# A hybrid streaming layer on one core: the sample tile's stage cut into twelve steps, and each tile's output transpositions placed behind the next tile's state product

## The chip, the core and the metric

The kernel runs on one core of a Trainium2 chip. A core has five engines that each work through a list of instructions of their own, in order: PE (TensorE, the matmuls), DVE (VectorE), ACT (ScalarE), POOL (GpSimd) and SP (SyncE, which here only issues DMAs). They wait for one another by semaphores. The metric is the device time of one execution in microseconds (us); the time of a kernel is the median of its runs.

## What is computed

One layer of a streaming encoder over 2048 prompt frames (16 tiles of 128) and 8 running streams of 16 frames (one more tile, number 16, the sample tile), width 1024, in float32. Cut to what matters here:

```python
h   = rmsnorm(x, norm_mix_pre)
P   = h @ w_in          # -> q|k|v (3*512), z (512), b (4), a (4), B, C, H (512 each)
qkv = silu(causal_dwconv(P[qkv], conv_prev, conv_qkv_w))      # 4 taps, 4 heads x 128
beta, g = sigmoid(b), -exp(a_log) * softplus(a + dt_bias)
# gated delta rule, in chunks: (I + A) is unit lower triangular
A   = strict_lower(kb @ k.T * decay)
u, w = solve(I + A, [v * beta, kb * exp(g)])
# along the chunks of a stream, with the state S (128 x 128 per head):
v_new = u - w @ S
o   = (q * exp(g)) @ S + (q @ k.T * decay) @ v_new
S   = S * exp(g_last) + k_tail.T @ v_new
o   = rmsnorm(o, gdn_norm_w) * silu(z)
y   = B * causal_dwconv(C * H)                                # 3 taps
x   = x + rmsnorm(concat(o, y) @ w_o)
x   = x + rmsnorm((silu(h2 @ w_gate) * (h2 @ w_up)) @ w_down) # h2 = rmsnorm(x)
```

The prompt's tiles carry S from one to the next; the sample tile has eight states of its own.

## The kernel before

**Phases.** The span has four: the w_in phase (0 to about 970 us), the w_o phase, gate and up (L1010), and down (L1168). The change is in the first.

**Groups.** The w_in phase takes the tiles in six groups, numbered 0 to 5: [0, 1, 16], [2, 3, 4], [5, 6, 7], [8, 9, 10], [11, 12] and [13, 14, 15]. Each goes through 28 projections (`project`, the matmuls at L139): one projection multiplies the group's tokens (384 columns, 256 in group 4) with one 128-wide slice of w_in, in 24 matmuls, since both sides are split into a `hi` and a `lo` part. Projections are counted through here, 0 to 167: group 1 has 28 to 55, and so on. In a group 0 to 11 give k, v, q (`qkv_stage`), 12 to 15 z (`z_stage`) and 16 to 27 the C, H and B of the short convolution (`sc_stage`).

**What a group does beside its projections.** `x_prep` takes the next group's x, gets each token's root mean square, spreads it over the partitions with a matmul with ones (`spread`, L179) and makes the eight pairs `hi` (ScalarE, L209) and `lo` (VectorE, L206 and L210). `gate_prep` makes b and a (the 16-wide matmuls with `wba`, also L139). `pair_stage` makes k k^T and q k^T per tile (L519, L520) and then the solve: 31 steps of two VectorE instructions (L539, L541) on all the group's 32-blocks at once; the result goes to DRAM (L542) and comes back in another layout (`utd`). `level_stage` builds the larger blocks out of it (PE at L568 to L595). `chunk_stage` does a prompt tile: S.k (L625), U.r (L632), the new state (L639), q.S (L646), qk.y (L651). `sample_stage` does the sample tile, head by head: L677, L679, L684, L687 and L693 on PE. Both end in `out_stage`: o is normalized (L612), transposed by PE (L615) and multiplied with `sz`, the SiLU of z, into `ot` (L617).

**What sets the order.** The program is traced in the order of the code, and a scheduler then puts each engine's list in order from its own estimate of times, with what was traced earlier first. All the stages of a group behind its k, v, q thus run among the projections of the next group. The engines keep that order on the chip.

**Walls.** Three PSUM banks hold projections (`dbank`), two the pair, level, chunk and sample products (`gbank`), one the q.S, qk.y and output transpositions (`obank`). `sz` has one buffer. A group's z projections 12 to 14 therefore fill the three banks and wait there until the last `out_stage` of the group before has read `sz`; the projection after them (projections 43, 71, 99, 127, 155 and the ones that follow each) cannot start sooner. The xk tiles, which also serve `rg` in `spread` and `bsb` in `gate_prep`, have four buffers.

## Time and profile before

| | |
|---|---|
| Time, median of 3 runs | 2603.46 us (2603.07 to 2608.24) |
| Profiled execution, its own time | 2609.88 us |
| Its span | 2608.1 us |
| Granted TensorE clock, mean over the span | 0.987 |
| PE busy | 2509.2 us (96%), in 15129 matmul records |
| VectorE busy | 1748.9 us (67%) |
| ScalarE busy | 1033.2 us (40%) |
| GpSimd busy | 645.1 us (25%) |

The span is one execution under the profiler, from its first instruction to its last, and the execution's own time is 1.8 us longer. [...]

### The profile page before, as it was taken

To read this page: it belongs to the slowest core of one execution; us is meant where nothing else is said; L and a number is where in the kernel's file an instruction comes from. 1 tells how busy PE (TensorE), PEld (TensorE's weight loads), DVE (VectorE), ACT (ScalarE), POOL (GpSimd) and SP (SyncE) were. 2 spreads that over 40 slices of the span, in tenths; PEclk is the share of its full clock that TensorE was granted. 3 is DMA by queue.
4 is the path that set the end of the run, shared out by engine and by line. 5 is a ranking of instruction groups with operands and counts; after the bars stand their busy time and mean duration, and the time that the engine had idled before them with its cause. 6 is when DMAs were issued, how large, how long until landed. Compare 5 with 4: busy or idle time off the path is not lost.

```text
span 2608.1 us, 41962 instructions
## 1 busy us (share of the span) xinstructions
PE 2509.2 (96%) x15129; PEld 2337.4 (90%) x15129; DVE 1748.9 (67%) x3549; ACT 1033.2 (40%) x2496; POOL 645.1 (25%) x598
## 2 busy tenths in 40 slices
PE   8989999999989999999999999999999999999998
PEld 7989899999888988778999999999999988788786
DVE  7787766666587665777878864544655555677598
ACT  6545144261554423444434442222433335333343
POOL 3321101010120101214556620000000025555563
PEclk9999999999999999999999999999999999999999
DMA  7876575757567573768877788887988853443466
GB/s 266 297 267 238 193 268 198 246 193 237 193 205 247 184 233 129 234 216 287 291 253 271 264 281 259 280 246 244 295 272 296 275 176 106 125 125 122 128 216 185
DMA packets 320816, 589.42 MB, mean 226 GB/s; under 512 B 55533, under 2 KB 204721, under 8 KB 301793
## 3 DMA queue, kind: packets, MB, share of 16 engines
q1 hardware_dynamic: 182512, 509.28, 58.8%
q10 hardware_dynamic: 138096, 77.46, 9.8%
q8 instruction: 120, 1.97, 0.3%
q14 instruction: 88, 0.71, 0.1%
HBM read 424.60 MB, written 162.05 MB: 225 GB/s over the span
## 4 chain that ended last, share of the span: by engine, by line
PE 70%; DVE 11%; DMA 9%; ACT 4%; issue 3%; POOL 2%; ACTq 1%; SPq 0%; DVEq 0%; POOLq 0%
PE fbank L1010 32%; PE dbank L139 15%; PE fbank L1168 10%; PE tbank L794 3%; PE dbank L794 3%; DMA xk<-in_xT 1%; DVE xr L1187 1%; DMA dr<-in_w_dn 1%; DVE acc L370 1%; DMA xt<-in_x 1%; DVE acc L1127 1%; DMA w<-wsplit 1%; DVE Ts L541 1%; DMA partd<-pt 1%; DMA utd<-sT 1%
## 5 line engine op out<-in xcount | busy, mean ns | idle before, releaser
L1010 PE MATMUL fbank<-xh,fw 128*128 128x384 f32 (+1 forms) x3696 | 901.3, 327 | 9.4 <-ACT m L1044 4.4
L139 PE MATMUL dbank<-hi,w 128*128 128x384 f32 (+1 forms) x2688 | 685.3, 334 | 12.7 <-ACT w L342 6.0
L1010 PEld LDWEIGHTS fbank<-xh,fw 128*128 128x128 f32 x3696 | 653.2, 188 | 11.3 <-ACT m L1044 5.0
L1010 PE MATMUL fbank<-xl,fw 128*128 128x384 f32 (+1 forms) x1848 | 603.7, 327 | 0.0
L139 PEld LDWEIGHTS dbank<-hi,w 128*128 128x128 f32 x2688 | 480.8, 191 | 18.5 <-ACT w L342 6.0
L1168 PE MATMUL fbank<-dw,as 128*128 128x512 f32 x1980 | 458.8, 393 | 8.6 <-DVE acc L1127 2.5
L1168 PEld LDWEIGHTS fbank<-dw,as 128*128 128x128 f32 x1980 | 370.6, 188 | 96.5 <-DVE acc L1127 4.5
L139 PE MATMUL dbank<-lo,w 128*128 128x384 f32 (+1 forms) x1344 | 446.4, 332 | 1.1 <-DVE lo L228 1.1
L1010 PEld LDWEIGHTS fbank<-xl,fw 128*128 128x128 f32 x1848 | 348.1, 188 | 0.0
L139 PEld LDWEIGHTS dbank<-lo,w 128*128 128x128 f32 x1344 | 256.9, 191 | 3.7 <-DVE lo L228 1.7
L1152 POOL TENSOR_TENSOR as<-ar,as 128x256 fp32r<-128x256 f32 (+1 forms) x207 | 186.5, 911 | 277.7 <-ACT as L1149 276.9
L1127 DVE TENSOR_TENSOR acc<-acc,fbank 128x512 f32<-128x512 f32 x248 | 166.3, 682 | 93.4 <-PE fbank L1168 75.6
L867 POOL TENSOR_TENSOR dw<-dr,dw 128x512 fp32r<-128x512 f32 x52 | 77.3, 1498 | 484.6 <-ACT dw L865 484.4
L1149 ACT CAST as<-ar 128x256 fp32r<-128x256 f32 (+1 forms) x288 | 117.8, 427 | 181.3 <-PE fbank L1168 130.0
L985 ACT CAST fw<-rg 128x512 fp32r<-128x512 f32 x124 | 77.3, 623 | 188.9 <-PE fbank L1010 170.8
L370 DVE SCALAR_TENSOR_TENSOR acc<-R,cw,acc 128x384 f32<-128x384 f32 (+2 forms) x216 | 132.8, 620 | 12.8 <-ACT acc L401 8.8
L344 POOL TENSOR_TENSOR w<-wr,w 128x512 fp32r<-128x512 f32 x49 | 73.0, 1490 | 228.0 <-ACT w L342 170.5
L1057 DVE TENSOR_TENSOR c<-u,fbank 128x384 f32<-128x384 f32 (+1 forms) x66 | 34.9, 529 | 102.2 <-PE fbank L1010 102.0
L1053 DVE TENSOR_TENSOR m<-m,m 128x384 f32<-128x384 f32 (+1 forms) x44 | 23.1, 525 | 97.8 <-ACT m L1046 97.8
L539 DVE TENSOR_TENSOR pr<-As,Ts 48x31 f32<-48x31 f32 (+25 forms) x186 | 66.7, 359 | 29.8 <-DMA As<-sa 25.7
L342 ACT CAST w<-wr 128x512 fp32r<-128x512 f32 x98 | 56.4, 616 | 61.9 <-PE dbank L139 29.4
L1055 ACT ACTIVATE m<-fbank 128x384 f32<-128x384 f32 (+1 forms) x66 | 31.2, 473 | 121.5 <-PE fbank L1010 112.4
(358 smaller groups left out, 3708.3 us busy)
## 6 DMA issues: line engine op xcount, KB each, us to landing
w<-wsplit SPq DMA_DIRECT2D x119, 1024.0 KB, 5.3
fw<-fsplit SPq DMA_DIRECT2D x188, 512.0 KB, 4.8
fsplit<-fw SPq DMA_DIRECT2D x94, 512.0 KB, 4.0
partd<-pt ACTq DMA_DIRECT2D x88, 384.0 KB, 6.5
rg<-in_w_gu SPq DMA_DIRECT2D x62, 512.0 KB, 4.3
wsplit<-w SPq DMA_DIRECT2D x28, 1024.0 KB, 5.3
wr<-in_w_in SPq DMA_DIRECT2D x98, 256.0 KB, 3.9
ar<-partd SPq DMA_DIRECT2D x48, 384.0 KB, 3.3
```

Source lines behind the costliest of these rows:

```text
L139: T.matmul(ps, l, r, start=(i == 0), stop=(i == n - 1))
L344: e.tensor_tensor(out=wl[:, c], in0=wr, in1=wh[:, c].bitcast(F32), op=ALU.subtract)
L370: V.scalar_tensor_tensor(acc, raw(d), w[:, d:d + 1], acc, op0=ALU.mult, op1=ALU.add)
L539: V.tensor_mul(p3, As[:m, j, j + 1:32].unsqueeze(2).broadcast_to([m, a, b]), Ts[:m, j, 0:b].unsqueeze(1).broadcast_to([m, a, b]))
L794: T.matmul(pss[n], m_[:, j, :], w_[k][:, n * 512:(n + 1) * 512], start=(k == 0 and ci == 0), stop=(k == KD - 1 and ci == 2))
L867: e.tensor_tensor(out=w[:, 1], in0=v, in1=w[:, 0].bitcast(F32), op=ALU.subtract)
L985: A.copy(w[:, 0], v)
L1010: T.matmul(ps, w_[:, c], b_[k][:, :hw], start=(first and k == 0 and ci == 0), stop=(k == KH - 1 and ci == 2), skip_group_check=not first)
L1127: V.tensor_add(dst, dst, ps)
L1149: ins = A.copy(a[:, 0, :n], v)
L1152: e.tensor_tensor(out=a[:, 1, :n], in0=v, in1=a[:, 0, :n].bitcast(F32), op=ALU.subtract)
L1168: T.matmul(ps, a[:, x_, q * P:(q + 1) * P], w[:, y_], start=(start and q == 0 and ci == 0), stop=(q == c - 1 and ci == 2), skip_group_chec ...
```

## The change

Three things. `x_prep` becomes a generator that is stepped between the projections of `sc_stage`, so that its instructions are traced among them and not behind them. `sample_stage` becomes a generator with three stops per head; its twelve steps are traced behind the first twelve projections of the next group, where before all of it stood in its own group behind `z_stage`. And a tile's `out_stage` is traced behind the next tile's state product, with PE's first transposition ordered behind that product (`issue_after`); the last tile's stands behind the first projection of `sc_stage`. The x and xk loads are ordered behind the same weight loads as before (`w0 + 11`, `w0 + 20`), xk now one load ahead. No instruction is added or taken away on any engine.

```diff
-        def x_prep(tiles):
+        def x_prep(tiles, got, w0):
...
                         A.activation(xt, xt, AF.Square, accum_out=ss[:, i:i + 1])
+                    yield
...
             rb = spread(r, n)
...
+            load()
+            yield
+            load()
             for k in range(KD):
...
+                got.append((h, l))
+                load()
+                yield
...
             fetch()
+            if steps and j < 12:
+                next(steps[0], None)
             return ps
...
             for h in range(H):
-                T.transpose(ps[:, h * P:(h + 1) * P], o[:, h, :], ident)
+                with tc.issue_after(after.ins) if after is not None and h == 0 else ExitStack():
+                    T.transpose(ps[:, h * P:(h + 1) * P], o[:, h, :], ident)
...
-                T.matmul(ps[:, h * P:(h + 1) * P], kl[:, h, :], yt[:, h, :], start=True, stop=True)
+                last = T.matmul(ps[:, h * P:(h + 1) * P], kl[:, h, :], yt[:, h, :], start=True, stop=True)
...
+            for f in outs:
+                f(last)
             ps = obank()
...
             qkv_stage(tiles, hi, lo, rb, gt, gp if (len(GROUPS) - gi) % 2 else dp)
+            while steps:
+                for _ in steps.pop():
+                    pass
...
-                    sample_stage(t, i, gt)
+                    for o in outs:
+                        o(None)
+                    outs = []
+                    steps.append(sample_stage(t, i, gt))
                 else:
-                    S = chunk_stage(t, i, gt, S)
-            sc_stage(tiles, hi, lo, rb)
+                    S, o = chunk_stage(t, i, gt, S, outs)
+                    outs = [o]
...
+            def step(b):
+                if b == 0:
+                    for o in outs:
+                        o(pmm[0])
+                if nxt is not None and b >= 2 * (MAXT - len(GROUPS[gi + 1])):
+                    next(nxt)
```

**Place 1: VectorE, end of group 0.** In the order of before, the last of the 31 solve steps of group 0 (L539 and L541 on `pr` and `Ts`) stand ahead of all of the x_prep of group 1 (L206 and L210 on `xk`, `lo`):

```order
L539 TENSOR_TENSOR pr<-As,Ts 48x60
L391 COPY R<-hist 128x3
L541 TENSOR_TENSOR Ts<-Ts,pr 48x2x30
L539 TENSOR_TENSOR pr<-As,Ts 48x31
L541 TENSOR_TENSOR Ts<-Ts,pr 48x31
L501 TENSOR_TENSOR yo<-acc,dbank 128x256
L543 COPY As<-Ts 48x32x32
L503 TENSOR_TENSOR yo<-acc,dbank 128x128
L206 TENSOR_TENSOR xk<-xk,rb 128x384 x2
L505 TENSOR_TENSOR yo<-yo,rb 128x384
L206 TENSOR_TENSOR xk<-xk,rb 128x384
L210 SCALAR_TENSOR_TENSOR lo<-xk,vec,hi 128x384 x3
```

In the changed kernel the same stretch reads as follows (L559 and L561 are the solve, L219 and L223 x_prep, L506 and L512 the u of the last short convolution); the last solve row, of 48x31, and the copy of `As` come 23 rows further on:

```order
L506 TENSOR_TENSOR u<-cs,dbank 128x256
L512 TENSOR_TENSOR u<-cs,dbank 128x8x16
L561 TENSOR_TENSOR Ts<-Ts,pr 48x10x22
L507 COPY shist<-u 128x2
L513 COPY sch<-u 128x16
L559 TENSOR_TENSOR pr<-As,Ts 48x207
L223 SCALAR_TENSOR_TENSOR lo<-xk,vec,hi 128x384
L561 TENSOR_TENSOR Ts<-Ts,pr 48x9x23
L387 SCALAR_TENSOR_TENSOR acc<-u,scw,acc 128x400
L223 SCALAR_TENSOR_TENSOR lo<-xk,vec,hi 128x384
L559 TENSOR_TENSOR pr<-As,Ts 48x192
L223 SCALAR_TENSOR_TENSOR lo<-xk,vec,hi 128x384
```

All of the x_prep of group 1 now stands ahead of the solve's end. On PE, the matmul of `spread` stands behind the 23rd projection instead of the 28th, and 13 of the 16 gate matmuls with `wba`, which read `hi` and `lo`, stand in one row behind the 28th, where they were mixed among projections 29 to 31.

**Place 2: PE ahead of projection 43 (the fourth z projection of group 1).** Before, the sample tile's third and fourth heads stand there alone (L677 and L679 are a head's first products, L693 its last):

```order
L693 MATMUL gbank<-ye,kls 128x512
L179 MATMUL tbank<-rg,cst 128x384
L693 MATMUL gbank<-ye,kls 128x512
L677 MATMUL gbank<-st,kz 128x128 x8
L679 MATMUL gbank<-st,qz 128x128 x8
L684 MATMUL gbank<-rs,ubuf_213 128x128
L687 MATMUL gbank<-yts,dt 128x128
L693 MATMUL gbank<-ye,kls 128x512 x2
L677 MATMUL gbank<-st,kz 128x128 x8
```

In the changed kernel (L699 and L701 first, L717 last) three heads follow one another there; the third of them is not shown:

```order
L636 MATMUL obank<-cst,o 128x128 x4
L717 MATMUL gbank<-ye,kls 128x512
L180 MATMUL tbank<-rg,cst 128x384
L717 MATMUL gbank<-ye,kls 128x512
L699 MATMUL gbank<-st,kz 128x128 x8
L701 MATMUL gbank<-st,qz 128x128 x8
L707 MATMUL gbank<-rs,ubuf_213 128x128
L711 MATMUL gbank<-yts,dt 128x128
L717 MATMUL gbank<-ye,kls 128x512 x2
L699 MATMUL gbank<-st,kz 128x128 x8
```

One head more runs with no projection left to fill its waits.

**Place 3: PE ahead of projection 127 (the fourth z projection of group 4; group 3's chunks end here).** Before, the last output transpositions of group 3 (L615) have everything else of the group behind them; the L646 that follows is already group 4's:

```order
L139 MATMUL dbank<-hi,w_8565 128x256
L615 MATMUL obank<-cst,o 128x128 x4
L452 MATMUL tbank<-cst,qT 128x128 x4
L646 MATMUL obank<-S,qT 128x128 x4
L139 MATMUL dbank<-hi,w_8859 128x256
```

In the changed kernel (L636 the output transpositions, L669 q.S, L674 qk.y, L540 and L539 the pair products) the second tile's output and the third tile's q.S, qk.y and output all stand there:

```order
L636 MATMUL obank<-cst,o 128x128 x4
L539 MATMUL gbank<-kT 128x128 x4
L469 MATMUL tbank<-cst,qT 128x128 x2
L540 MATMUL gbank<-qT,kT 128x128 x4
L469 MATMUL tbank<-cst,qT 128x128 x2
L669 MATMUL obank<-S,qT 128x128 x4
L469 MATMUL tbank<-cst,qT 128x128 x2
L180 MATMUL tbank<-rg,cst 128x384
L674 MATMUL obank<-yt,dt 128x128 x4
L636 MATMUL obank<-cst,o 128x128 x4
L669 MATMUL obank<-S,qT 128x128 x4
L139 MATMUL dbank<-hi,w_8859 128x256
```

Between the last qk.y and the transpositions that need its result nothing else is left on PE. The first level products of group 4 (L568) also move, from 15.4 projections behind this place to 12.2.

Two more shifts of PE's list are too spread out to be shown as a few rows. Ahead of projection 71, where group 1's third tile ends, its state product stands a quarter of a projection (six matmuls) later than before, and between that and its qk.y stand eight more pair products and six projection matmuls less. In group 3, the first transpositions of k (L427) stand 15 projection matmuls later than before.

## Rows read from the trace of the kernel before

**Rows 1.** The page: busy time of each engine, and the chain that ended last.

```profile
PE 2509.2 (96%) x15129; PEld 2337.4 (90%) x15129; DVE 1748.9 (67%) x3549; ACT 1033.2 (40%) x2496; POOL 645.1 (25%) x598
...
PE 70%; DVE 11%; DMA 9%; ACT 4%; issue 3%; POOL 2%; ACTq 1%; SPq 0%; DVEq 0%; POOLq 0%
```

**Rows 2.** Windows: length, busy PE, PEld, DVE, ACT, POOL, granted clock, DMA share, GB/s.

```profile
123.00:165.00 42.00, 36.33 (x207) 35.34 (x205) 40.68 (x110) 9.31 (x16) 13.53 (x7) 0.96 0.93 328
160.00:175.00 15.00, 7.52 (x31) 6.51 (x32) 11.64 (x34) 4.37 (x9) 2.80 (x4) 0.66 0.87 291
...
675.00:690.00 15.00, 11.19 (x153) 9.41 (x152) 9.28 (x25) 5.74 (x14) 0.19 (x1) 0.89 0.51 159
690.00:765.00 75.00, 67.41 (x548) 65.38 (x547) 57.19 (x165) 49.84 (x141) 21.01 (x19) 0.96 0.57 190
```

**Rows 3.** Waits of PE, 0 to 1010 us: for what; total, times, longest.

```profile
PE tbank L139 <- ACT hi L209: 12.0, 4, 8.0
```

**Rows 4.** Windows of L206, then of L210, on VectorE: busy, records, clock.

```profile
166.00:182.00 16.00, 4.33 (x8) 0.81 0.47 131
...
166.00:182.00 16.00, 4.75 (x8) 0.81 0.47 131
```

**Rows 5.** Timeline of SP and ACT behind the solves of groups 0 and 4: start, duration.

```profile
164.73 0.32 SPq L542 DMA_DIRECT2D sT<-Ts  x1
...
174.69 1.23 ACT L573 COPY AU<-utd 32x128 f32<-32x128 f32 x4 [1.22 <-DMA utd<-sT]
...
812.97 0.32 SPq L542 DMA_DIRECT2D sT<-Ts  x1
...
818.58 0.61 ACT L573 COPY AU<-utd 32x128 f32<-32x128 f32 x2 [6.41 <-DMA utd<-sT]
```

**Rows 6.** Timeline of VectorE and PE at the start of group 1; brackets: waited before.

```profile
161.25 0.40 DVE L487 TENSOR_TENSOR u<-cs,dbank 128x256 f32<-128x256 f32 x1
...
167.34 0.50 PE L139 MATMUL tbank<-hi,wba 128*16 128x384 f32 x1 [7.98 <-ACT hi L209]
...
172.33 0.51 PE L139 MATMUL dbank<-hi,w 128*128 128x384 f32 x2
...
186.14 0.67 PE L589 MATMUL gbank<-AU 64*64 64x64 f32 x8
```

**Rows 7.** Windows of L139 alone on PE: length, busy, records, clock.

```profile
297.00:309.00 12.00, 12.00 (x71) 1.00 0.51 173
...
766.00:776.00 10.00, 9.81 (x80) 1.00 0.67 203
```

**Rows 8.** The sample tile's third head: window (as Rows 2), then PE rows.

```profile
270.16:277.91 7.75, 6.43 (x41) 4.74 (x40) 5.12 (x10) 0.67 (x3) 0.58 (x2) 1.00 0.50 154
...
294.64 0.42 PE L139 MATMUL dbank<-hi,w 128*128 128x384 f32 x1
```

**Rows 9.** Timeline of PE at projection 71.

```profile
447.85 1.05 PE L651 MATMUL obank<-yt,dt 128*128 128x128 f32 x8
...
454.95 0.66 PE L615 MATMUL obank<-cst,o 128*128 128x128 f32 x4 [3.21 <-DVE o L612]
...
458.17 0.67 PE L139 MATMUL dbank<-hi,w 128*128 128x384 f32 x1
```

**Rows 10.** Timeline of PE, projections 84 to 127, and the level products of group 4.

```profile
540.96 0.55 PE L427 MATMUL tbank<-cst,kraw 128*128 128x128 f32 x3 [1.70 <-DVE tl L307]
...
677.48 0.65 PE L589 MATMUL gbank<-AU 64*64 64x64 f32 x8 [1.45 <-DVE AU L584]
...
683.88 0.29 PE L139 MATMUL tbank<-hi,wba 128*16 128x256 f32 x1 [2.36 <-ACT hi L209]
...
722.43 1.09 PE L615 MATMUL obank<-cst,o 128*128 128x128 f32 x4 [3.48 <-DVE R L391]
...
757.15 1.06 PE L520 MATMUL gbank<-qT,kT 128*128 128x128 f32 x8
...
762.09 0.44 PE L452 MATMUL tbank<-cst,qT 128*128 128x128 f32 x2 [2.17 <-ACT junkq L412]
```

More of the change, by code (lines that the diff above doesn't have):

```diff
@@ L138, in mm3 @@
         for i, (l, r) in enumerate(pairs):
-            T.matmul(ps, l, r, start=(i == 0), stop=(i == n - 1))
+            m = T.matmul(ps, l, r, start=(i == 0), stop=(i == n - 1))
+        return m
     ps_o, ps_a = ExitStack(), ExitStack()
@@ L191, in x_prep @@
                     xt = cp.tile([P, D // 2], F32, tag="x", name="xt")
-                    with tc.issue_after(wloads[-20 + 2 * i + q].ins):
+                    with tc.issue_after(wloads[w0 + 11 + 2 * i + q].ins):
                         nc.sync.dma_start(out=xt, in_=x[t, :, q * 512:(q + 1) * 512])
@@ L200, in x_prep, with load @@
             rb = spread(r, n)
-            hi, lo = [], []
+            yield
+            xks = []
+            def load():
+                k = len(xks)
+                if k < KD:
+                    xk = cp.tile([P, W1], F32, tag="xk", name="xk", bufs=XKB)
+                    with tc.issue_after(wloads[w0 + 20 + k].ins):
+                        nc.sync.dma_start(out=xk[:, :c], in_=xT[k, :, tiles[0] * P:tiles[0] * P + c])
+                    xks.append(xk)
+            load()
+            yield
+            load()
             for k in range(KD):
-                xk = cp.tile([P, W1], F32, tag="xk", name="xk", bufs=XKB)
-                with tc.issue_after(wloads[-11 + k].ins):
-                    nc.sync.dma_start(out=xk[:, :c], in_=xT[k, :, tiles[0] * P:tiles[0] * P + c])
+                xk = xks[k]
                 V.tensor_mul(xk[:, :c], xk[:, :c], rb[:, :c])
@@ L324, in gate_prep @@
             return dict(sb=sb, eG=eG, tl=tl, eL=eL, eLs=eLs, dt=dts)
+        steps = []
+        pmm = []
         wloads = []
@@ L685, in sample_stage @@
                 A.copy(yt[:, h, :], ps[:, :P])
+                yield
                 ps = bank()
@@ L738 @@
         for gi, tiles in enumerate(GROUPS):
-            if gi:
-                hi, lo, rb = *x_prep(tiles), None
             gt = gate_prep(tiles, hi, lo, rb)
             qkv_stage(tiles, hi, lo, rb, gt, gp if (len(GROUPS) - gi) % 2 else dp)
+            while steps:
+                for _ in steps.pop():
+                    pass
             pair_stage(tiles, gi, gt)
@@ L745 @@
             z_stage(tiles, hi, lo, rb, gt)
+            outs = []
             for i, t in enumerate(tiles):
                 if t == SAMPLE:
-                    sample_stage(t, i, gt)
-                else:
-                    S = chunk_stage(t, i, gt, S)
-            sc_stage(tiles, hi, lo, rb)
+                    for o in outs:
+                        o(None)
+                    outs = []
+                    steps.append(sample_stage(t, i, gt))
+                else:
+                    S, o = chunk_stage(t, i, gt, S, outs)
+                    outs = [o]
+            nxt, got = None, []
+            if gi + 1 < len(GROUPS):
+                nxt = x_prep(GROUPS[gi + 1], got, 28 * gi)
+            def step(b):
[4 more added lines that the diff above has]
+                    next(nxt)
+            sc_stage(tiles, hi, lo, rb, step)
+            if nxt is not None:
+                for _ in nxt:
+                    pass
+                hi, lo = ([v[q] for v in got] for q in range(2))
+                rb = None
             if SAMPLE in tiles:
```

20 lines of the change are left out of this document (11 added, 9 removed).

## The prediction, made before the changed kernel ran

> **What bounds the kernel.** I began with the busy times and the chain that ended last [rows 1]. PE is busy for 96% of the span and holds 70% of the chain, so no other engine is the bound as a whole: VectorE, the next, has 67%. The change adds no instruction and takes none away, so PE's work stays what it is, and the only thing to win or lose is the time in which PE stands still or runs at its lower clock. The question is at which places that time lies and whether the new order reaches it. I then read the waits of PE in the w_in phase, and PE's timeline at the places where its order changes.
>
> The largest single stop is the start of group 1. PE has finished the 28th projection and stands for 7.98 us before its first gate matmul, for the `hi` of L209 [rows 6]; four such waits make 12.0 us in the whole phase [rows 3]. Why is `hi` late? Between 123 and 165 us VectorE is busy for 40.68 of 42.00 us [rows 2], which is the solve of group 0, and only when the solve is stored (164.73) [rows 5] do the x_prep rows come. So here VectorE bounds, and only what comes off it or goes ahead of something on it counts.
>
> [...]
>
> **A, start of group 1.** x_prep is 8 rows of L206, 4.33 us, and 8 of L210, 4.75 us [rows 4]: 9.1 us, which now stand ahead of the solve's end. VectorE was full, so the solve ends 9.1 us later: its store moves from 164.7 to 173.8. From store to the block copies on ScalarE it takes 5.6 us in group 4 (812.97 to 818.58) and 10.0 in group 0 (164.73 to 174.69) [rows 5]. So level products can start between 179.4 and 183.8.
>
> When does PE get there? The 13 gate matmuls in one row need the sixth `lo`. Adding the durations of before along VectorE's new order, the last u of the short convolution (161.25 before [rows 6]) comes 2.3 us later, since seven L206 and three L210 stand ahead of it and fewer solve rows do; from it to the sixth `lo` are 12 rows of 4.1 us. That is 167.6, nearly the 167.34 of before. So the stop does not go, it ends at the same time. What changes is that PE has done 13 gate matmuls by then and does no level work in between. To where the first level products now stand are 69 projection matmuls at 0.17 us (71 in 12.00 us [rows 7]), 11.7 us, some six gate matmuls not yet done or left over, 0.8, and the slow stretch, 2.4: 182.5. In before the same point of the projections lies four matmuls ahead of 186.14 [rows 6], at 185.4, of which 0.4 is level work that the changed kernel has still to do. **A is 185.0 - 182.5 = 2.5 us won.** Bounds: 1.2 if the data come only at 183.8; 5.6 if PE is early and 179.4 decides.
>
> **B, the sample tile.** One head more runs alone. Such a head takes 7.75 us, of which PE is busy for 6.43 [rows 8]; among projections the other 1.3 were filled. **B is 1.3 us lost.** Bounds: nothing, if its waits overlap those of another head; 3.9, half of 7.75, if the longer stretch of small products brings the lower clock.
>
> **C, projection 71.** The third tile's state product comes six matmuls later, 1.0 us. From there to its qk.y there are eight more pair products, 1.05 us at the 1.05 us per 8 records of such a group [rows 9], and six projection matmuls less, -1.0. From qk.y to the output transposition PE waits on VectorE and ScalarE: 447.85 to 454.95, 7.1 us, and then 3.2 to projection 71 at 458.17 [rows 9]. These do not change, so the projection comes 1.0 later. **C is 1.1 us lost**; bounds nothing, and 3.2, the wait shown at 454.95, once over.
>
> **D, start of group 3.** The first k transposition waits 1.70 us [rows 10]. It now stands 15 projection matmuls later, 15 x 0.17 = 2.6 us, which covers that. **D is 1.7 us won**; at worst nothing.
>
> **E, group 4.** The waits at 677.48, 683.88, 722.43 and 762.09 are 1.45, 2.36, 3.48 and 2.17 us [rows 10], 9.5 in sum. In the new order other matmuls stand where they were: the output transpositions of 722.43 are behind the next state product, the gate rows and the last q transpositions elsewhere. The lower clock goes with the stops: 0.89 over 15 us and 0.96 over 75 us [rows 2] are 1.7 and 3.0 us. Against this 14.2 stands a new stop. Ahead of projection 127 nothing lies between the third tile's qk.y and its output, and by the same chain as under C that is 7.1 us from the start of a product that takes 1.05 [rows 9], so 6.0 of standing, and 1.7 of slow clock behind it. E would be 6.5 won at projection 127.
>
> Then the level products of group 4 stand 3.2 projections earlier. The last pair products start at 757.15 [rows 10] and the solve is stored at 812.97 [rows 5], 55.8 us; by the durations along VectorE's order its solve stretch is 4.2 us shorter now (41.7 to 37.5), and with 5.6 from store to copies the data come 57.2 us behind the pair products. PE's work in between is 10.3 us from qk.y to the next projection (447.85 to 458.17), about 2 for what stands ahead of qk.y, and 299 matmuls at 0.123 (80 in 9.81 us [rows 7]), 36.8, with 1.7 of slow clock: 50.8. PE would wait 6.4 and give all of it back. It gives nothing back if the solve, which finds VectorE idle in a part of that stretch, closes up. I take half: **E is 3.2 us won**, bounds 0 and 6.5.
>
> **The rest** has the same counts in another order (groups 2, 3 and 5, and the w_o phase); I take nothing for it, with 3 us either way, about a wait such as that of 722.43. SP's x loads hang behind the same weight loads; one xk load ahead takes one of the four buffers sooner, and a weight load queued behind it on SP would wait for it. Before, no row shows SP held up that way; I cost it at nothing, since the loads of weights run two projections ahead.
>
> **Sum.** 2.5 - 1.3 - 1.1 + 1.7 + 3.2 = 5.0 us won. Against the profiled execution that is 2609.9 - 5.0 = 2604.9. That execution lies 6.4 us above the median of the runs, 2603.46; I take the same 5.0 from the median: **2598.5 us**. The three runs of before lie within 5.2 us, 0.2%, and that is also about what a measurement of this kernel can tell from no change.
>
> **Rivals.**
>
> *The chains close up.* Data that PE waits for come at the short ends: level products of group 0 at 179.4 (A 5.6), projection 71 not later (C 0), E whole at 6.5. For it: VectorE has over 30% idle in the span [rows 1], and the waits of 3.21 at 454.95 and 3.48 at 722.43 were for VectorE rows that a better order can bring sooner. Against: between 123 and 165 us it has none. 5.6 - 1.3 + 1.7 + 6.5 = 12.5: 2591.0.
>
> *It does nothing in the end.* The stops change places only: the level products' data decide at both places (A 1.2, E 0): 1.2 - 1.3 - 1.1 + 1.7 = 0.5, so 2603.0. For it: every long stop is the end of a chain over VectorE that the change doesn't shorten.
>
> *Slower: the solve is late all the way.* The 9.1 us of x_prep ahead of the solve delay everything behind it, level, chunk and sample stages of group 0, up to projection 43, which in before starts at 294.64 [rows 8] and then comes 9.1 later; A is then -9.1. It decides from the point where the chain from the solve to that projection has less spare time than 9.1 minus what A saves on PE. Against it: from 270 us on PE is busy with the sample heads for 6.43 of 7.75 us [rows 8], so there PE's own work and not the solve sets the pace. -9.1 - 1.3 - 1.1 + 1.7 + 3.2 = -6.6: 2610.1. [...]
>
> **How the numbers follow.** Forecast 0.40, with a range of its own of 2594 to 2603; chains close up 0.24; nothing in the end 0.16; slower 0.20. The range for 8 in 10 reaches from 2587 (the first rival, with the 3 us of the rest) to 2611 (the last, with 1 more). Faster by over 0.2%, that is below 2598.3: half of the forecast's chance and all of the first rival, 0.44. Slower, above 2608.7: 0.20 and a little of the third case, 0.21. The rest, 0.35, is within.
>
> **What would show it.** In the changed profile: PE's wait ahead of the first gate matmul of group 1 ends near 167 to 168 us, and the store of group 0's solve is issued near 174 (A); three heads of about 7.7 us follow one another ahead of projection 43 (B); projection 71 starts about as far behind its qk.y, 10 us, as before (C); the 1.70 at L427 is gone (D); the waits at 677 to 762 us are replaced by one of about 6 us ahead of projection 127, and L568 of group 4 waits 3 us or so (E). I am wrong if the stop of 8 us goes altogether, if L568 of group 1 waits for the solve for more than 2 us, if projection 43 starts later than 294 us, or if a weight load on SP is held behind an xk load.

## The result, and the profile after

The changed kernel took 2617.51 us (median of four runs, 2614.64 to 2619.88) where the kernel before took 2605.24 in the same comparison: a ratio of 1.0035 with a 95% interval of 1.0018 to 1.0052. By the ratio it is slower by some 9 us; the two medians, of four runs each, lie 12.3 us apart. I had forecast 2598.5, a gain of 5, and the time lies outside the range given.

The page of the changed kernel's profiled execution (2614.64 us, span 2612.9), for [rows 1]: engines' busy time, then the chain.

```profile
PE 2514.4 (96%) x15129; PEld 2339.7 (90%) x15129; DVE 1751.1 (67%) x3549; ACT 1032.2 (40%) x2496; POOL 644.0 (25%) x598
...
PE 43%; DVE 8%; DMA 3%; issue 2%; POOL 1%; ACT 1%; ACTq 1%; SPq 0%; DVEq 0%; POOLq 0%
```

The busy times are those of before: no work came or went. The chain's shares are no measure of the loss, since the chain could be followed back over less of the span. The waits of PE from 0 to 1015 us in the changed kernel (for what; total, times, longest), for [rows 3]:

```profile
PE obank L636 <- DVE o L632: 10.0, 2, 5.8
PE tbank L452 <- DVE kt L448: 7.2, 7, 2.5
...
PE gbank L717 <- DVE ye L715: 3.7, 4, 1.6
PE tbank L139 <- DVE lo L223: 3.6, 4, 2.1
...
PE tbank L139 <- ACT hi L222: 2.6, 3, 1.4
...
PE gbank L717 <- DVE xss L200: 1.8, 1, 1.8
```

The 12.0 us of waits for `hi` are down to 2.6, with 3.6 for `lo`. Two outputs now cost 10.0 us of waiting, where two cost 6.7 before, and the k transpositions (`kt`) 7.2, where it was 4.3. Added up over all of PE's rows up to projection 167, its waits are 47.9 us in both kernels (44.3 and 49.4 in the second execution of each list, see below). The stops have moved, and there is no less of them.

Where the time went is best seen by the places at which a projection starts. The next list is worked out from the starts of the matmuls of L139 in each trace (24 to a projection). It gives the time in us from one projection to another, and from projection 167 to the first matmul of gate and up. The labels are those of the experiments below. "Before again" is a second execution of the same kernel. The kernel g5 has the changed list through all 168 projections, and g3 and f1 have it up to projection 112. The line of p2 comes from its second run, since the execution of it that was profiled first took 6348.7 us.

```
                28-43   43-71   71-99   99-127  127-155  167-gate/up
before          127.0   163.5   159.6   146.5   137.8    245.3
before again    128.6   162.3   158.0   149.9   134.8    244.9
changed         129.6   165.5   155.0   152.0   138.2    248.0
changed (g5)    134.2   165.6   155.1   149.6   135.2    247.1
g3              131.6   165.2   156.5   150.7   138.7    248.1
f1              130.1   165.3   156.1   152.6   135.8    245.3
p1  x_prep      136.3   166.4   158.0   144.9   136.1    246.2
p2  sample      130.3   158.8   159.6   152.8   136.4    245.2
p3  outputs     133.2   162.3   158.4   147.9   139.2    248.8
p12             126.7   165.8   155.7   150.8   139.4    246.6
p23             137.0   164.7   160.7   150.3   137.6    247.3
n3              127.0   159.2   160.5   152.6   137.9    249.5
n4              127.7   160.5   154.5   153.5   136.9    249.8
n6              132.2   160.2   160.5   149.1   137.6    248.7
n7              126.6   161.3   156.1   147.4   136.3    246.1
a4              132.6   169.4   154.7   150.7   138.9    250.9
a6              133.9   165.3   157.0   149.6   138.6    247.9
```

One list repeats itself within 0.4 to 4.6 us in these columns: 146.5 and 149.9 us from 99 to 127 are the same kernel before.

In the changed kernel's own profile PE runs ahead and falls back. It is 11.7 us ahead of before at projection 40 and 0.9 behind at 43; it is 2.6 ahead at 98, 8.7 ahead at 126 and 3.8 behind at 127. Most of that lead is no gain: the new list puts work behind these projections that stood ahead of them before, 70 matmuls (of the sample's heads above all) behind projection 40 and 50 behind projection 126. The windows from 99 to 126 and from 126 to 127 show it, those of before first (length, busy PE, PEld, DVE, ACT, POOL, clock, DMA share, GB/s):

```profile
617.73:753.79 136.06, 126.83 (x1026) 122.23 (x1025) 93.92 (x265) 60.03 (x156) 20.02 (x20) 0.97 0.66 216
753.79:764.19 10.40, 8.23 (x64) 7.76 (x62) 7.11 (x22) 5.07 (x24) 2.04 (x2) 0.93 0.59 190
...
616.01:745.10 129.09, 120.82 (x977) 115.79 (x975) 87.76 (x251) 56.44 (x145) 17.74 (x18) 0.99 0.68 223
745.10:767.97 22.87, 15.38 (x115) 13.88 (x113) 17.33 (x56) 9.17 (x41) 5.27 (x5) 0.90 0.38 128
```

From 99 to 126 PE gains 7.0 us, and 6.0 of them are busy time that comes back behind 126.

**The start of group 1.** PE, SP and ScalarE of the changed kernel, for [rows 5, 6]: gate matmuls, the store of the solve, the block copies, the first level products.

```profile
163.38 0.35 PE L139 MATMUL tbank<-lo,wba 128*16 128x384 f32 x1 [2.12 <-DVE lo L223]
...
165.90 0.43 PE L139 MATMUL dbank<-hi,w 128*128 128x384 f32 x1
...
172.93 0.32 SPq L562 DMA_DIRECT2D sT<-Ts  x1
...
179.20 1.21 ACT L593 COPY AU<-utd 32x128 f32<-32x128 f32 x4
...
180.58 0.44 PE L588 MATMUL gbank<-utd,AU 32*32 32x32 f32 x16
```

The stop of 7.98 us is now one of 2.12 and two short ones, and the solve is stored at 172.93, 8.2 later than before. The windows show the same (length, busy PE, PEld, DVE, ACT, POOL, clock, DMA share, GB/s), for [rows 2]:

```profile
123.00:165.00 42.00, 38.06 (x214) 35.62 (x212) 41.52 (x104) 12.75 (x23) 10.38 (x6) 1.00 0.95 341
160.00:175.00 15.00, 11.77 (x58) 9.91 (x56) 13.34 (x40) 2.76 (x5) 0.00 (x0) 0.89 0.72 273
```

**Projection 43.** PE of the changed kernel, then VectorE, for [rows 8]:

```profile
258.04 1.10 PE L717 MATMUL gbank<-ye,kls 128*128 128x512 f32 x2 [1.77 <-DVE xss L200]
260.47 0.88 PE L180 MATMUL tbank<-rg,cst 128*128 128x384 f32 x2 [1.34 <-DVE rg L177]
262.33 1.12 PE L717 MATMUL gbank<-ye,kls 128*128 128x512 f32 x2 [0.97 <-DVE ye L715]
263.29 1.95 PE L699 MATMUL gbank<-st,kz 128*128 128x128 f32 x16
...
271.02 2.02 PE L699 MATMUL gbank<-st,kz 128*128 128x128 f32 x16 [0.37 <-DMA st<-in_state]
...
278.42 2.02 PE L699 MATMUL gbank<-st,kz 128*128 128x128 f32 x16
...
295.50 0.44 PE L139 MATMUL dbank<-hi,w 128*128 128x384 f32 x1
```

```profile
256.27 0.69 DVE L196 SCALAR_TENSOR_TENSOR xt<-xt 128x512 f32<-128x512 f32 x1 [1.29 <-DMA xt<-in_x]
256.89 0.08 DVE L196 DVE_READ_ACCUMULATOR xt<-xt 128x1 f32 x1
256.89 0.75 DVE L638 SCALAR_TENSOR_TENSOR ot<-obank,vec,sz 128x512 f32<-128x512 f32 x1
...
261.58 0.69 DVE L715 TENSOR_TENSOR ye<-yts,cst 128x512 f32<-128x512 f32 x1 [1.25 <-DMA mixd<-ot]
```

Three heads follow one another and start 7.7 and 7.4 us apart. Ahead of them the end of the first head waits three times on VectorE, 4.1 us in sum (two such waits, 1.6 us in sum, stand there in before): VectorE stands for a load of x, then does the last output (`ot`), and the head's second `ye`, which shares its buffer with `ot`, waits until that output is stored.

**Projection 71** in the changed kernel, for [rows 9]:

```profile
450.46 1.06 PE L674 MATMUL obank<-yt,dt 128*128 128x128 f32 x8
...
456.58 1.09 PE L636 MATMUL obank<-cst,o 128*128 128x128 f32 x4 [4.16 <-DVE o L632]
...
461.05 0.67 PE L139 MATMUL dbank<-hi,w 128*128 128x384 f32 x1
```

**Projections 112 to 127** in the changed kernel, PE with VectorE and ScalarE, for [rows 10]. First the first chunk's round, then a k transposition, then the end:

```profile
697.43 1.16 PE L646 MATMUL gbank<-S,kT 128*128 128x128 f32 x8
...
701.14 1.31 DVE L359 TENSOR_TENSOR w<-wr,w 128x512 fp32r<-128x512 f32 x1 [2.52 <-issue]
...
702.44 0.68 DVE L648 TENSOR_TENSOR r<-gbank,eG 128x512 f32<-128x512 f32 x1
...
708.93 0.63 ACT L198 ACTIVATE xt<-xt 128x512 f32<-128x512 f32 x1 [3.39 <-DMA xt<-in_x]
...
709.55 0.57 ACT L655 COPY yt<-gbank 128x512 f32<-128x512 f32 x1
...
715.11 0.44 PE L452 MATMUL tbank<-cst,kt 128*128 128x128 f32 x2 [2.18 <-DVE kt L448]
...
757.31 1.16 PE L674 MATMUL obank<-yt,dt 128*128 128x128 f32 x8 [0.22 <-DVE sqe L628]
...
761.62 0.18 DVE L559 TENSOR_TENSOR pr<-As,Ts 32x31 f32<-32x31 f32 x1 [2.43 <-DMA As<-sa]
...
763.47 0.69 DVE L632 TENSOR_TENSOR o<-o,ofr 128x512 f32<-128x512 f32 x1
...
764.31 1.09 PE L636 MATMUL obank<-cst,o 128*128 128x128 f32 x4 [5.84 <-DVE o L632]
...
767.97 0.56 PE L139 MATMUL dbank<-hi,w 128*128 128x256 f32 x1
```

The first S.k of group 3 starts at 697.43. In before it starts at 695.79 and its `r` on VectorE follows at 697.21 (the timeline of before):

```profile
695.79 1.16 PE L625 MATMUL gbank<-S,kT 128*128 128x128 f32 x8
...
697.21 0.62 DVE L627 TENSOR_TENSOR r<-gbank,eG 128x512 f32<-128x512 f32 x1
```

PE is 7.7 us ahead at projection 116, and yet the chain of chunks begins 1.6 later. In the changed kernel `r` then stands behind a weight row and comes 5.0 us behind the start of S.k, where it was 1.4; both repeat in the second execution of each list.

This chain starts with the group's first level products, here in before, before again, the changed kernel and g5:

```profile
659.86 0.44 PE L568 MATMUL gbank<-utd,AU 32*32 32x32 f32 x16
...
658.45 0.44 PE L568 MATMUL gbank<-utd,AU 32*32 32x32 f32 x16
...
659.15 0.44 PE L588 MATMUL gbank<-utd,AU 32*32 32x32 f32 x16
...
664.59 0.44 PE L588 MATMUL gbank<-utd,AU 32*32 32x32 f32 x16
```

From there to projection 127 (764.19, 766.20, 767.97 and 771.32) it takes 104.3 and 107.7 us in before, 108.8 and 106.7 in the changed list.

### The profile page after: what moved, and what is told of

It reads as the page before. It is cut to its first block, busy times and chain, and to the rows that moved or that the text cites. A ratio compares the mean times of both kernels' runs of the same rounds, so it can differ in the third digit from the quotient of the medians.

```text
span 2612.9 us, 41968 instructions
## 1 busy us (share of the span) xinstructions
PE 2514.4 (96%) x15129; PEld 2339.7 (90%) x15129; DVE 1751.1 (67%) x3549; ACT 1032.2 (40%) x2496; POOL 644.0 (25%) x598
## 4 chain that ended last, share of the span: by engine, by line
PE 43%; DVE 8%; DMA 3%; issue 2%; POOL 1%; ACT 1%; ACTq 1%; SPq 0%; DVEq 0%; POOLq 0%
PE fbank L1057 30%; PE fbank L1215 10%; PE tbank L841 1%; PE dbank L841 1%; DVE acc L1174 1%; DVE xr L1234 1%; DMA dr<-in_w_dn 1%; DMA partd<-pt 1%; POOL dw L914 1%; DVE fw L1033 0%; DVE dw L914 0%; ACTq L1131 0%; DVE acc L1231 0%; DMA fh<-hTd 0%; DVE as L1199 0%
## 5 line engine op out<-in xcount | busy, mean ns | idle before, releaser
L139 PE MATMUL dbank<-hi,w 128*128 128x384 f32 (+1 forms) x2688 | 683.9, 334 | 12.0 <-ACT w L357 5.8
L139 PEld LDWEIGHTS dbank<-hi,w 128*128 128x128 f32 x2688 | 482.3, 192 | 18.1 <-ACT w L357 5.8
L139 PE MATMUL dbank<-lo,w 128*128 128x384 f32 (+1 forms) x1344 | 446.9, 333 | 0.0
L139 PEld LDWEIGHTS dbank<-lo,w 128*128 128x128 f32 x1344 | 257.4, 191 | 1.6 <-DVE lo L241 0.3
L559 DVE TENSOR_TENSOR pr<-As,Ts 48x31 f32<-48x31 f32 (+25 forms) x186 | 63.6, 342 | 27.3 <-DMA As<-sa 23.2
```

Of the source, the lines that this page charges most:

```text
L139: m = T.matmul(ps, l, r, start=(i == 0), stop=(i == n - 1))
L559: V.tensor_mul(p3, As[:m, j, j + 1:32].unsqueeze(2).broadcast_to([m, a, b]), Ts[:m, j, 0:b].unsqueeze(1).broadcast_to([m, a, b]))
```

## The experiments

**One part at a time.** p1 keeps the stepped x_prep alone, p2 the sample steps alone, p3 the deferred outputs alone; p12 keeps x_prep and the sample steps, p23 the sample steps and the outputs. The parts that are not kept are undone like this (p2, p3 and p23 also load xk as before, which is cut here):

```diff
 # p1, p2, p12, g5 for the last group, g3 for group 3: outputs not deferred
-                    S, o = chunk_stage(t, i, gt, S, outs)
-                    outs = [o]
+                    S, o = chunk_stage(t, i, gt, S, [])
+                    o(None)
 # p1, p3: sample stage in one piece
-                    steps.append(sample_stage(t, i, gt))
+                    for _ in sample_stage(t, i, gt):
+                        pass
 # p2, p3, p23: x_prep behind the short convolution
-                if nxt is not None and b >= 2 * (MAXT - len(GROUPS[gi + 1])):
-                    next(nxt)
```

p1: 

> The x_prep of the next group stepped among the projections, the sample stage and the outputs as before. If x_prep is the cause (its rows stand ahead of the solve on VectorE and its squares wait for loads ahead of the copies of the chunk chain on ScalarE), this part alone carries the loss: projection 127, which starts at 764.2 us in the profile of before and 768.0 in the changed kernel, starts at 767 or later, and the time is 7 to 10 us above before. If the deferred outputs are the cause, group 4 here runs as in before or better: projection 127 at or before 764, and the time within 4 us of before. In both, the stop of 8 us ahead of the first gate matmul of group 1 shrinks to 2 or 3 us, and projection 43 comes within 1.5 us of the 294.6 of before, since the sample heads stand alone there.

p2: 

> Only the sample stage cut in twelve steps. Its order on PE differs from before by little (the third head moves a few tenths of a projection). Theory of x_prep and theory of the outputs: within 3 us of before, projection 43 at 294.6 plus 0 to 2, projection 127 within 2 of 764.2. If the sample steps are the cause, projection 43 comes 4 us or more later and the time is 5 us or more above before.

p2 once more: 

> The sample steps alone once more, for a profile: by its time of 0.3% above before it should lose some 8 us; at projection 43 if it is the sample heads (294.6 in before, then 299 or later), spread over 71, 99 and 127 if it is the new order of the other groups.

p3: 

> Only the outputs deferred behind the next tile's state product. If the deferral is the cause, the chain from a group's last state product over two outputs through one bank is longer, PE stands at projection 127 for about 6 us as in the changed kernel (there 5.84), projection 127 starts at 767 or later and the time is 7 us or more above before. If x_prep is the cause: projection 127 at 764 plus or minus 2, and the time within 4 us of before. Projection 71, 458.2 in before and 461.0 in the changed kernel, moves with the deferral alone in both theories, to 460 or 461.

p23: 

> The changed kernel with x_prep traced behind the short convolutions as before. Its list on PE is that of before up to the start of group 2 but for the outputs and the sample steps, and from the fourth group on it is that of the changed kernel. If x_prep is the cause through its trace position, the time falls back to within 4 us of before. If what counts is the list of group 4 (equal here), projection 127 comes as late behind the start of group 4 as in the changed kernel (92.8 us behind projection 112, before 86.0) and the time is 6 us or more above before.

p12: 

> The changed kernel with every output traced as in before. If the deferral costs by itself, the time is 3 us or more below the changed kernel, at 2614 or less; if each list is a draw, anywhere from 2607 to 2626. By the list, projection 127 has to wait for the third tile's q.S, qk.y and output all the same, so a stop of 4 us or more stays there.

Measured, as ratios to before: p1 1.0034 (1.0021 to 1.0047), p2 1.0031 (1.0018 to 1.0044), p3 1.0051 (1.0032 to 1.0070), p12 1.0029 (1.0017 to 1.0042), p23 1.0093 (1.0073 to 1.0113). Each part alone loses as much as all three together, and x_prep, which loses 9 us alone, saves some 15 when it is added to the two others (p23 against the whole). So the parts don't add up, and none of them is "the" cause. Nor do the places fit: p2 has no edit behind group 1, and 99 to 127 takes it 152.8 us, the means being 148.2 in before and 150.8 in the changed list; p1, which I suspected there, has the shortest such stretch of all, 144.9, though its projection 127 starts at 771.1 for what it lost before 43. In p2's profile projection 43 starts at 298.5, which is 3.9 or 2.4 late by the two executions of before. In p12 the stop ahead of projection 127 stays (4.8 us), as its list said. Only one stretch separates by a part, and by no more than 0.5 us, where two executions of before differ by 1.3: 43 to 71 takes 165.2 to 169.4 us in every kernel with the stepped x_prep (the highest is a4 below) and 158.8 to 164.7 in all others, the two with the z projections last left out; 71 to 99, with 154.7 to 158.0 against 154.5 to 160.7, gives a part of it back.

**One place at a time, in the changed kernel.** g3 and g5 leave the outputs of one group alone as they were; f1 orders the solve behind the last output's normalization:

```diff
-            V.tensor_mul(o, o, bc(f))
+            normed[:] = [V.tensor_mul(o, o, bc(f))]
...
-                V.tensor_mul(p3, As[:m, j, j + 1:32].unsqueeze(2).broadcast_to([m, a, b]),
-                             Ts[:m, j, 0:b].unsqueeze(1).broadcast_to([m, a, b]))
+                with tc.issue_after(normed[0].ins) if normed and j == 0 else ExitStack():
+                    V.tensor_mul(p3, As[:m, j, j + 1:32].unsqueeze(2).broadcast_to([m, a, b]),
+                                 Ts[:m, j, 0:b].unsqueeze(1).broadcast_to([m, a, b]))
```

g3: 

> The changed kernel, but the outputs of group 3 alone (those worked on ahead of projection 127) stand as in before, not behind the next tile's state product. Up to projection 117 the lists are the same. In the changed kernel projection 127 starts 92.8 us after projection 112 (before 86.0). If the deferred output is what makes that chain longer, the third tile's q.S and qk.y no longer queue behind the second tile's output, the stop of 5.84 us shrinks by the 2 to 4 us that one output takes, and projection 127 comes 88 to 90 us after projection 112; the time falls by 2 to 4 us. If the pace is that of the rounds of S.k, U.r and state product, which VectorE and ScalarE serve late, projection 127 stays within 1 us of 92.8 and the time within 2 us of the changed kernel.

g5: 

> The changed kernel, with the outputs of the last group alone as in before. From the last projection to the first matmul of the feed-forward phase the profiles show 245.4 us in before and with the x_prep or sample part alone (246.4, 245.4), 248.2, 248.9 and 247.5 wherever the outputs are deferred. If the deferral costs there, this stretch falls back to 245.5 to 246.5 and the time by 2 to 3 us; if not, it stays above 247.5.

f1: 

> The changed kernel, with the first row of each solve on VectorE ordered behind the normalization of the last output before it. Ahead of projection 127 that row stood in front of the output's sum of squares and waited 2.43 us for its load, and the output's normalization came 2.7 us behind its last square (1.2 to 1.6 where no such row stands there). If VectorE's order sets the stop, the normalization follows within 1.7 us and projection 127 comes 1 to 2 us earlier behind projection 112 (91 to 92 instead of 92.8); the time falls by 1 to 2 us or stays. If the chain is bound elsewhere, 92.8 stays.

g3: projection 127 comes 92.6 us behind 112 and the ratio is 1.0042 (1.0029 to 1.0056). Its stop is 4.1 us in place of 5.8, with a new one of 1.4 ahead of the third tile's qk.y: without the deferred output PE waits about as long, at two places, and projection 127 comes no sooner. g5: 247.1 us from projection 167 to gate and up, 1.0039 (1.0026 to 1.0053). It is 0.9 less than in the changed kernel, not the 2 to 3; and n3, n4 and n6, which defer nothing, have 248.7 to 249.8 there, and f1, which defers all of them, has 245.3, so that theory fell. f1: 91.6 us, 1.0039 (1.0024 to 1.0053). VectorE and PE of f1 at that place (L561 the solve, L634 the normalization, L638 the output):

```profile
766.92 0.69 DVE L634 TENSOR_TENSOR o<-o,ofr 128x512 f32<-128x512 f32 x1 [0.75 <-POOL ofr L133]
767.53 0.17 DVE L561 TENSOR_TENSOR pr<-As,Ts 32x31 f32<-32x31 f32 x1
...
767.76 1.09 PE L638 MATMUL obank<-cst,o 128*128 128x128 f32 x4 [4.82 <-DVE pr L561]
```

The stop is 4.82 us in place of 5.84, so VectorE's order made one microsecond of it (g5, with the changed list there, has 5.79). The 91.6 us tell nothing, since the changed list itself has 92.7 and, in g5, 90.4. From 99 to 127 f1 takes 152.6 us, more than either, so the microsecond is not seen in the time.

**The z projections moved last.** In both kernels, the four z projections stand behind the twelve of the short convolution (in the changed one `sc_stage` takes its `step` along, and the last tile's output stands right behind the chunks):

```diff
-        order = [(j, gi) for gi in range(len(GROUPS)) for j in range(28)]
+        order = [(j, gi) for gi in range(len(GROUPS)) for j in (*range(12), *range(16, 28), *range(12, 16))]
...
-            z_stage(tiles, hi, lo, rb, gt)
             ...
             sc_stage(tiles, hi, lo, rb)
+            z_stage(tiles, hi, lo, rb, gt)
```

Before: 

> The kernel before with the four z projections of each group moved behind the twelve of the short convolution, so that they no longer stop at projections 43, 71, 99, 127 and 155 for the outputs of the group before. If those places are where PE loses its time (11.7, 7.9 and 4.3 us at 43, 71 and 127, counted over its usual pitch), 10 to 20 us go, and the sample tile's third and fourth heads run among projections. If the chain of VectorE behind the pair products sets the pace wherever the z stand, the wait comes back at the next place and the time is within 4 us of before.

Changed: 

> The changed kernel with the same move of the z projections. Where the theory of the stops ahead of the z projections holds, the early gains of the change (PE is 9.4 us ahead at projection 39, 8.7 at 126) have no place left where they are given back, and this comes out 5 us or more below z_last_before. If it is the chain itself that the change makes longer, it stays 5 us or more above z_last_before, with a stop at projection 139, where the outputs of group 3 now end.

Both lost: 1.0168 (1.0155 to 1.0181) and 1.0108 (1.0095 to 1.0121). But the changed one is 0.60%, or 15.6 us, faster than the other, more than the 5 us that I had set for the theory of the stops: with the z projections there, the change gains. Whether that is the wall or again the list, this one pair doesn't tell. In the first the stop at 43 is gone, 28 to 43 takes 98.7 us and the sample heads run among projections. But projection 167 comes 6.5 us later than in before, and from there to gate and up it takes 274.4 us instead of 245.3. The waits of PE, 0 to 1240 us, in the first:

```profile
PE tbank L139 <- ACT hi L209: 16.3, 5, 7.5
PE dbank L139 <- DMA w<-wsplit: 10.3, 7, 3.9
PE dbank L139 <- ACT acc L401: 8.9, 4, 3.9
PE obank L615 <- DVE o L612: 8.4, 2, 5.0
```

The stop comes back at other places, and the last group's chain falls out of the projections into the w_o phase. Moving the wall has not shortened the whole.

**Edits without a purpose.** By then every list had been slower than that of before. Four edits to the kernel before, and the first two of them to the changed kernel, ask whether any new list is:

```diff
 # n4, a4                     # the other half of x squared on VectorE
-                    if q:
+                    if not q:
 # n6 (a6: w0 + 12)           # x loads one weight load later
-                    with tc.issue_after(wloads[-20 + 2 * i + q].ins):
+                    with tc.issue_after(wloads[-19 + 2 * i + q].ins):
 # n7                         # xk loads one weight load later
-                    with tc.issue_after(wloads[-11 + k].ins):
+                    with tc.issue_after(wloads[-10 + k].ins):
 # n3                         # level stage traced behind z
-            level_stage(tiles, gt)
             z_stage(tiles, hi, lo, rb, gt)
+            level_stage(tiles, gt)
```

n4: 

> The kernel before with one edit that moves nothing on purpose: in x_prep the square of the first half of x goes to VectorE and that of the second to ScalarE, where before it is the other way round. The scheduler's lists change over the whole first phase all the same, about as much as with each part of the change alone. If the loss of each part (9, 8 and 13 us, more than the whole) comes from what the part does, this one is within 3 us of before. If the list of before is simply a favourable one, which any new list loses, this one is 5 to 12 us slower too, with the loss at projections 43, 71 or 127.

n6: 

> The kernel before with the x loads of x_prep ordered one weight load later, again an edit without a purpose, that changes the lists about as much. By what the edit does: within 3 us of before, since x is used 10 projections later. By the theory of the favourable list: 5 to 12 us slower.

n3: 

> The kernel before with the level stage traced behind the z projections instead of ahead of them, a third edit that does nothing to the work. Theory of the favourable list: 4 to 14 us slower than before, as the two others (5.5 and 13.8). Theory that parts of the change cost by what they do: within 3 us.

n7: 

> The kernel before with the xk loads of x_prep ordered one weight load later. Favourable list: 4 to 14 us slower. Otherwise within 3 us, or slower only at the starts of the groups, where x_prep waits for those loads.

a4: 

> The changed kernel with the swap of the squares, which cost the kernel before 5.5 us. If the lists of before and of the change are draws from about the same spread, this lies anywhere from 2 us below to 8 above the changed kernel (2610 to 2626), overlapping with the edited lists of before. If the change itself costs 9 us, this lies at 2617 or above, 9 us above the swapped kernel before (2612).

a6: 

> The changed kernel with the x loads ordered one weight load later, which cost the kernel before 13.8 us. Draws of one spread: 2610 to 2626, that is below or near the 2621 of the same edit of before. A cost of the change itself: 9 us above that, 2630.

Before again: 

> The kernel before once more. The same list: projections 43, 71, 99 and 127 within 1.5 us of 294.6, 458.2, 617.7 and 764.2 if a profile's marks can be trusted to that; if the stretch from 28 to 43 varies as in the four kernels that share the changed list there (129.6 to 134.2), projection 43 may lie up to 4 us off.

Ratios to before: n4 1.0021 (1.0011 to 1.0032), n6 1.0053 (1.0040 to 1.0065), n3 1.0035 (1.0021 to 1.0049), n7 0.9997 (0.9987 to 1.0008), a4 1.0057 (1.0038 to 1.0075), a6 1.0054 (1.0038 to 1.0070). Three of four edits that do nothing to the work cost 5 to 14 us, and the change's 9 lies among them. n7 costs nothing, though its VectorE list is as new as the others' (compared in order up to projection 167, 56% of its rows match those of before, 48 to 60% in the other three), so not every new list loses, and none here gains. With the change each edit reads 0.36% more (n4 to a4) and 0.01% more (n6 to a6). a4, at 2624.8, fits both expectations, which overlap there (2610 to 2626, and 2617 or above), though it lies above every run of its partner n4; a6, at 2622.7, lies where one spread had it, and not at 2630. With the z projections last, the change read 0.60% less. The second execution of before starts projections 43, 71, 99 and 127 at 296.1, 458.3, 616.3 and 766.2: the first three within the 1.5 us that I had set, the last 2.0 late.

No kernel that ran is faster than before by more than the noise.

## Why the prediction was wrong, by its steps

Measured against the two executions of before (means) and those of the changed list (four up to projection 112: the changed kernel, g3, g5 and f1; two from there on, the changed kernel and g5; behind projection 167 the changed kernel alone):

**A and B, 1.2 us won; measured 3.0 lost at projection 43** (298.3 against 295.4). A's mechanism was right: the solve is stored at 172.93 (I had 173.8), the copies run at 179.20 (179.4 at the earliest), and the level products start at 180.58 where I had 182.5. It was under-sized: the 16 gate matmuls wait 3.2 us in all, since the `lo` come one after another among the solve's rows and the last wait ends at 165.5, not 167.6. The changed kernel does not show the 2.4 us of slow stretch in A's sum: its granted clock reads 0.51, 0.50, 0.50 and 0.79 in the four us from 166, in sum 1.7 us short of full clock, where in before it reads 0.52 over the 4.99 us from 167.34 to 172.33, 2.4 us short. But by B's place the lead is gone: from 28 to 43 the changed list takes 131.4 us where before takes 127.8 (means), though 12 matmuls fewer stand there. B was mis-sized. From projection 40 to 43 PE stands still for 8.3 us where it stood for 4.6 (7.7 in g5 and 4.5 in before again), so some 3.7 and not 1.3. The head itself cost what I had put down, 1.3 us of waits; the other 2.5 are the waits on VectorE ahead of the heads, 4.1 in place of 1.6, for which I had no term: I had moved the x_prep of group 1 in my sum and not that of group 2, nor the last output, past the sample's rows on VectorE.

**C, 1.1 lost; measured 2.5** (43 to 71: 165.4 against 162.9). From qk.y to the projection it takes 10.6 us, as I had it (10.3). What I missed is that qk.y itself comes later, counted from projection 43: by 1.8 us in the changed kernel (155.0 against 153.2) and 2.0 by the means, not 1.1. It needs the one output bank, in which the second tile's deferred output now stands ahead of q.S. That this is the cost is not shown, and two runs speak against it: p3, which has the deferred outputs, needs 162.3 from 43 to 71, and p12, which has none, has its qk.y 155.0 us behind projection 43 too.

**D, 1.7 won; measured 3.1** (71 to 99: 155.7 against 158.8). The stop of 1.70 is gone, as forecast, and so are the small ones beside it: PE waits 2.7 us from 71 to 98 in before and not at all in the changed kernel.

**E, 3.2 won, of it 6.5 at projection 127 and half given back behind it; measured 2.6 lost there** (99 to 127: 150.8 against 148.2; two executions of one list differ by 2.3 and 3.4 us here, so the gain is refuted, and the loss is not clear of that spread). This is the step that failed. "E would be 6.5 won at projection 127" took 9.5 us of waits and 4.7 of slow clock out of PE's time and put a new stop of 6.0, with 1.7 of slow clock, in. The four old waits did go and the new one is 5.84, but the step let nothing stand in the old ones' place. By it, 1.9 us of small waits would be left beside the new stop; the changed kernel has 9.9 (the longest are the 2.18 at 715.11, 1.63 and 1.14) and g5 9.1. All of PE's waits from 99 to 127 add up to 15.8 and 14.9 us in the changed list, where they were 11.4 and 12.5, and the granted clock over the stretch is 0.97 and 0.98, where it was 0.97 and 0.95.

Why did others come? PE's stops in this stretch are the end of a chain that runs over VectorE, ScalarE and PE in turn: level products, three rounds of S.k, r, U.r, yt, state product, then the outputs. It takes 104.3 and 107.7 us to projection 127 before and 108.8 and 106.7 in the changed list. So it is not shorter, and a stop that is taken out of PE's list in one place comes up in another; g3 and f1, which each shorten the 5.8, bring projection 127 no earlier than g5 has it (92.6 and 91.6 us behind projection 112, 90.4 in g5). That the chain is longer is not clear of the spread of one list. Only its first part is, up to S.k: 38.3 and 38.6 us against 35.9 and 35.8. Behind it, short rows of the chain do stand behind rows that wait for something else: `r` behind a weight row, `yt` behind a square of x that waited 3.39 us for its load, the last normalization behind a solve row that waited 2.43. But from S.k to projection 127 the changed list takes 70.5 and 68.1 us and before 68.4 and 72.0, so no loss is shown to come of them; only the last was tried by a run (f1), and it made one microsecond of the stop. The wait of 3 us or so that I had put ahead of group 4's first level products, to give half of E back, is not there: they start at 811.05 without one.

I had counted what a row on VectorE does to the rows behind it for a rival about the solve alone, and not for the rows of the chain that E runs over: `r`, at 702.44, comes right behind the weight row of 701.14, which takes 1.31 us.

**The rest, 0 with 3 either way; measured 2.9 lost** from projection 167 to gate and up (248.0 against 245.1). n3, n4 and n6 lose 3.6 to 4.7 there, and f1, with all of the change, 0.2, so this too comes with the list and is tied to no part of the change.

The sum of these is 3.0 + 2.5 - 3.1 + 2.6 + 2.9 = 7.9 us lost; 127 to 155 adds 0.4 (136.7 against 136.3). The measured ratio, 1.0035, says 9.1.

**The rivals.** None was right. "It does nothing in the end" had the mechanism, stops that only change places (47.9 us of waits up to projection 167 in both kernels), but not the loss. "The solve is late all the way" had nearly the time (2610.1), but not the way there: the level products, 180.58, did not wait for the late solve, and what came late at projection 43 was the sample's heads.

**What stays open.** That the change's loss is within what a new list of the scheduler costs without any purpose is shown. How much of the 9 us is the change's own is not: with the same edit made to both kernels, one pair says all of it (n4 and a4), one none (n6 and a6), and one that the change gains 15.6 us (z last). That before is a list chosen among many would explain why three of four idle edits lose and none gains; no run here shows how it was made.

## What to carry to other kernels

Before adding up stops that an edit removes from the busiest engine, find the chain that ends at the next place where that engine must wait, and ask whether the edit makes that chain shorter; if not, what is won ahead of it comes back as waits, there or on the way (here PE's waits up to projection 167 are 47.9 us in both kernels). And before calling an engine ahead at some point, count the work that stands behind that point now and stood ahead of it before. Where a scheduler writes the lists, time two or three edits that do nothing before giving a few tenths of a per cent to an edit that does something: here they cost from -0.03 to 0.53%. And cost a moved step by the rows that now stand ahead of a short row of the chain, on each engine, above all rows that wait for a load: at projection 43 three waits on VectorE's order cost 2.5 us more than before, and one solve row, put out of the way in f1, took one microsecond off a stop.

## What the runs showed that I had not expected

One list of instructions does not take the same time at all places: the four kernels that share the changed list up to projection 112 need 129.6, 131.6, 134.2 and 130.1 us from projection 28 to 43, but 165.2 to 165.6 from 43 to 71 and 155.0 to 156.5 from 71 to 99. And an edit that only moves a load by one weight load changed the time by 0.53% in one place (x, n6) and not at all in another (xk, n7).
